# A prefix log-sum-exp over 4 x 4096 rows: other tile heights, another order around the short tiles, other loads by rows

## Chip, core and metric

The kernel runs on one core of one Trainium2 chip. The metric is the device time of one execution in microseconds (us). A profiled execution also has a span: from its first to its last instruction.

## What is computed

The input x has shape (4, 4096, 4128), float32. Along the second axis the output is the running log-sum-exp:

```python
def reference(x):
    B, S, D = x.shape
    out = np.zeros_like(x)
    out[:, 0, :] = x[:, 0, :].copy()
    for t in range(1, S):
        mx = np.maximum(out[:, t - 1, :], x[:, t, :])
        out[:, t, :] = mx + np.log(np.exp(out[:, t - 1, :] - mx) + np.exp(x[:, t, :] - mx))
    return out.astype(np.float32)
```

So out[b, t, d] = log(sum over s <= t of exp(x[b, s, d])).

## The kernel before

**Tiles.** The 4096 rows of each of the 4 batches are cut into tiles of 2 or 3 times 128 rows: partition p of a tile holds 2 or 3 rows that follow one another (`r`), each 4128 numbers wide. The lists `begin` (first batch), `usual` (the two in the middle) and `final` (the last batch) say which tile has how many rows (L176 to L178); there are 46 tiles in all, ten of 2 rows and 36 of 3. A tile lives in one of four SBUF slots (`slots`), in turn, and is worked on in place: loaded, turned into exponentials, into prefix sums, into logarithms, and stored from the same slot.

**Chunks.** A tile's columns are cut into three chunks of 1376. Each chunk goes through these steps; the line is that of the instruction in the profile:

- `exp` (ScalarE, L113): Exp over the chunk's 2 or 3 rows.
- `sums` (VectorE, L133 for 3 rows, L135): the sum of the rows in each partition. For chunks 0 and 1 it goes into a buffer of its own, z0 or z1; for chunk 2 (called passed) it stays in the last row.
- `head` (TensorE, L142): a matmul with a triangular matrix makes, for each partition, the sum of all partitions above it, and of what is carried from the tile before. The result lies in one of two PSUM buffers, in turn.
- `add` (VectorE, L157 and L165, or L160 in a batch's last tile; L150 for chunk 2): adds this to the rows.
- `log` (ScalarE, L173 and L174; L169 for chunk 2): Ln of the rows.
- `fold` (VectorE, L123): brings chunk 2's carry from the tile before into the first row of the next. In a batch's first tile there is none; there `least` (L116) takes a minimum for each of the three chunks, and after a batch's last tile `total` (L126) takes a sum. These feed a check of the number range at the end (L297 to L312), which can send the kernel to a slower general path.

**Order.** The order on each engine is written out by hand, in lists: `act` for ScalarE, `vec` for VectorE, `pe` for TensorE, `move` for the DMA issues, all of them from SP. Each engine works through its list strictly in order. In turn t the ScalarE list has the three Ln of tile t, and the Exps of tile t + 1 placed between them; the VectorE list has the three adds of tile t, with sums of tile t + 1 between them. How many, the pair `turns[t]` says: its first part counts the Exps of tile t + 1 that are placed ahead of Ln 0, ahead of Ln 1, ahead of Ln 2 and behind it; its second part does the same for the sums, ahead of the adds. Where `turns` has no entry the pair is `usual_turn = (0, 2, 3, 3), (0, 0, 1, 1)`. What is not placed ahead comes at the start of the next turn.

**Moves.** SP first issues the loads of tiles 0 to 3. Then, from tile 1 on, each store of a tile t is followed by the load of tile t + 3, which goes into the slot of tile t - 1 and so has to wait until that tile's store has landed. The very last load is issued right behind the last but one. A store waits for the tile's last Ln. A load is one DMA for the whole tile (L93), or, for the tiles chosen by `BY_ROW`, one DMA for each of its rows (L96): before, these are tiles 0 to 6. All loads and stores run on one DMA queue in the order of their issue.

Of the kernel before, what the change touches and what calls it, by code (L numbers as in the profile page):

```python
# [13 lines left out]
MM = 512  # L14
NC = 3
SLOTS = 4
BY_ROW = 7
PASSED = NC - 1
SMALL = 2.0 ** -63
LARGE = 2.0 ** 62  # L20
# [3 lines left out]
def kernel(  # L24
# [57 lines left out]
    class Step:  # L82
# [6 lines left out]
            return rows.rearrange("(p j) d -> p j d", j=self.r)  # L89

        def load(self):
            if self.n >= BY_ROW:
                nc.sync.dma_start(out=self.xt, in_=self.dram(x))  # L93
                return
            for j in range(self.r):
                nc.sync.dma_start(out=self.xt[:, j, :], in_=self.dram(x)[:, j, :])  # L96
# [76 lines left out]
            nc.scalar.activation(e, e, ACT.Ln)  # L173
            nc.scalar.activation(self.row[r - 1], self.z, ACT.Ln)  # L174

    begin = [2, 2, 3, 3, 3, 3, 3, 3, 3, 3, 2, 2]  # L176
    usual = [2, 3, 3, 3, 3, 3, 3, 3, 3, 3, 3]
    final = [2, 3, 3, 3, 3, 3, 3, 3, 3, 2, 2, 2]  # L178
    steps = []
    for b in range(B):  # L180
        row = 0
# [9 lines left out]
    n = len(steps)  # L191
# [3 lines left out]
    for t in range(n):  # L195
# [8 lines left out]
    lists = {"move": moves, "act": [], "vec": [], "pe": []}  # L204
    act, vec, pe = lists["act"], lists["vec"], lists["pe"]
    usual_turn = (0, 2, 3, 3), (0, 0, 1, 1)
    turns = {
# [4 lines left out]
        n - 3: ((0, 0, 3, 3), (0, 0, 0, 0)),  # L212
        n - 2: ((1, 2, 3, 3), (0, 0, 1, 1)),
    }
    given = {"exp": [0] * n, "sums": [0] * n}
# [158 lines left out]
```

## Time and profile before

| what | value |
|---|---|
| median of three timed runs | 1266.24 us (1265.36 to 1266.4) |
| the profiled execution | 1262.61 us |
| its span | 1260.6 us |
| VectorE busy | 1047.2 us, 83% |
| ScalarE busy | 926.1 us, 73% |
| TensorE matmul busy | 601.3 us, 48% |
| read from and written to HBM | 270.53 MB each |
| mean rate of the DMA engines over the span | 429 GB/s |
| DMA issues: stores, whole loads, loads of one row | 46, 39, 19 |

The medians and the profiled execution are different executions of the same program. In the views of the profile, an instruction's line begins with its start and its length in us, or, in groups, with the source line and engine; `out<-in` names what is written and read; `x108` is a count; behind the bar a group has its busy time and the mean of one in ns, and the idle time of the engine before them with what ended it. A waits line reads: who waited for whom, us in total, times, the longest.

### The profile page before, as it was taken

Reading aid. Unit: us, or ns where it says so; the run is one execution under the profiler, and the core shown is the slowest. Engines: PE = TensorE matmul, PEld = TensorE weight load, DVE = VectorE, ACT = ScalarE, POOL = GpSimd, SP = SyncE. Lnnn points to the kernel's source line nnn. Section 1 sums busy time; section 2 is a strip of 40 time slices with the busy share of each in tenths; the row PEclk is TensorE's granted clock in tenths of the full one; section 3 lists DMA queues with packets and bytes.
Section 4 is the critical chain, followed back from the end, with each engine's and each line's share of the span. In section 5 each row is a group of like instructions: output and inputs, shape, how many; then the busy total and the mean of one; then the engine's idle time right before and its main releaser. Section 6 shows DMA issues by size and latency. Waiting matters only on the chain.

```text
span 1260.6 us, 3131 instructions
## 1 busy us (share of the span) xinstructions
PE 601.3 (48%) x830; PEld 233.9 (19%) x830; DVE 1047.2 (83%) x547; ACT 926.1 (73%) x369; POOL 3.8 (0%) x15
## 2 busy tenths in 40 slices
PE   3544444464545444445444544455454454445662
PEld 1221111121222111111111211121121121111220
DVE  4999888895899877888978978888897797888984
ACT  5968777776678677777857777777776677777882
POOL 1000000000000000000000000000000000000000
PEclk9866666676677676666765666666675666666676
DMA  9999999999999999999999999999999999999998
GB/s 398 426 441 427 428 435 434 424 434 431 438 434 429 425 443 434 429 428 436 429 442 428 439 432 428 433 442 429 429 435 426 434 412 442 430 429 433 430 423 375
DMA packets 14994, 541.28 MB, mean 429 GB/s; under 512 B 1664, under 2 KB 1664, under 8 KB 1664
## 3 DMA queue, kind: packets, MB, share of 16 engines
q1 hardware_dynamic: 14976, 541.07, 99.7%
q8 instruction: 7, 0.11, 0.0%
q14 instruction: 11, 0.09, 0.0%
HBM read 270.53 MB, written 270.53 MB: 429 GB/s over the span
## 4 chain that ended last, share of the span: by engine, by line
DMA 61%; ACT 22%; DVE 9%; issue 6%; SPq 1%; ACTq 0%; DVEq 0%
DMA x<-in_x_dram 57%; ACT x L113 11%; ACT x L169 5%; ACT x L173 4%; DMA out_dram<-x 4%; DVE x L150 2%; ACT x L174 2%; DVE x L157 2%; DVE z L135 1%; DVE x L133 1%; DVE z L160 1%; DVE x L135 0%; DVE x L123 0%; SPq L99 0%; DVE short L116 0%
## 5 line engine op out<-in xcount | busy, mean ns | idle before, releaser
L113 ACT ACTIVATE x<-x 128x4128 f32<-128x4128 f32 (+1 forms) x138 | 462.3, 3382 | 183.7 <-DMA x<-in_x_dram 183.6
L142 PE MATMUL p<-z,carried 128*128 128x512 f32 (+1 forms) x504 | 375.2, 910 | 456.4 <-DVE z L135 297.0
L173 ACT ACTIVATE x<-x 128x2752 f32<-128x2752 f32 (+1 forms) x92 | 206.0, 2239 | 129.7 <-DVE z L165 117.1
L133 DVE TENSOR_TENSOR x<-x 128x1376 f32<-128x1376 f32 x108 | 171.2, 1585 | 146.8 <-ACT x L113 146.8
L142 PEld LDWEIGHTS p<-z,carried 128*128 128x128 f32 x504 | 145.8, 309 | 687.4 <-DVE z L135 331.6
L142 PE MATMUL p<-x,summed 128*128 128x512 f32 (+1 forms) x276 | 194.3, 867 | 130.9 <-issue 125.1
L157 DVE TENSOR_TENSOR x<-p,x 128x2752 f32<-128x2752 f32 (+1 forms) x92 | 248.2, 2698 | 0.9 <-PE p L142 0.8
L150 DVE SCALAR_TENSOR_TENSOR x<-p,inner,x 128x4128 f32<-128x4128 f32 (+1 forms) x46 | 193.1, 4198 | 0.6 <-PE p L142 0.5
L135 DVE TENSOR_TENSOR z<-x 127x1376 f32<-127x1376 f32 x92 | 146.3, 1590 | 39.5 <-ACT x L113 33.7
L169 ACT ACTIVATE x<-x 128x4128 f32<-128x4128 f32 (+1 forms) x46 | 155.5, 3379 | 2.4 <-DVE x L150 2.4
L165 DVE TENSOR_TENSOR z<-x 128x1376 f32<-128x1376 f32 x84 | 133.8, 1592 | 2.9
L174 ACT ACTIVATE x<-z 128x1376 f32<-128x1376 f32 x92 | 122.7, 1333 | 0.0
L142 PEld LDWEIGHTS p<-x,summed 128*128 128x128 f32 x276 | 75.3, 290 | 248.5 <-issue 245.9
L135 DVE TENSOR_TENSOR x<-x 128x1376 f32<-128x1376 f32 x46 | 73.2, 1590 | 1.2
L123 DVE TENSOR_TENSOR x<-p,x 1x1376 f32<-1x1376 f32 x42 | 66.1, 1573 | 2.8 <-ACT x L113 2.4
L142 PE MATMUL p<-z,below 128*128 128x512 f32 (+1 forms) x48 | 31.9, 827 | 48.4 <-DVE z L135 28.7
L142 PEld LDWEIGHTS p<-z,below 128*128 128x128 f32 x48 | 12.7, 280 | 66.6 <-issue 31.0
L116 DVE TENSOR_REDUCE short<-x 1x1 f32<-1x1376 f32 x12 | 18.7, 1566 | 0.0
L160 DVE CUSTOM_DVE_ANT_0 z<-x 128x1376 f32<-128x1376 f32 x8 | 12.7, 1592 | 0.3
L126 DVE TENSOR_REDUCE probe<-p 1x1 f32<-1x1376 f32 x4 | 6.3, 1568 | 0.0
L308 PE MATMUL good<-ones,low 128*1 128x1 f32 x2 | 0.2, 164 | 5.5 <-DVE low L306 5.5
L74 POOL MEMSET z<- 128x1376 f32 x2 | 2.5, 1258 | 0.0
(21 smaller groups left out, 4.8 us busy)
## 6 DMA issues: line engine op xcount, KB each, us to landing
out_dram<-x SPq DMA_DIRECT2D x36, 6192.0 KB, 26.0
x<-in_x_dram SPq DMA_DIRECT2D x31, 6192.0 KB, 40.1
out_dram<-x SPq DMA_DIRECT2D x10, 4128.0 KB, 22.0
x<-in_x_dram SPq DMA_DIRECT2D x19, 2064.0 KB, 28.2
x<-in_x_dram SPq DMA_DIRECT2D x8, 4128.0 KB, 34.7
```

The costliest lines, as they stand in the source:

```text
L113: nc.scalar.activation(self.e, self.e, ACT.Exp)
L123: nc.vector.tensor_tensor(out=to, in0=pt[0:1], in1=to, op=ALU.add)
L133: nc.vector.tensor_tensor(out=e[1], in0=e[0], in1=e[1], op=ALU.add)
L135: nc.vector.tensor_tensor(out=self.z[0:n], in0=e[r - 2][0:n], in1=e[r - 1][0:n], op=ALU.add,)
L142: nc.tensor.matmul(self.pt[:, a:b], lhsT=w, rhs=self.z[:, a:b], start=True, stop=True,)
L150: nc.vector.scalar_tensor_tensor(out=self.e, in0=base, scalar=inner[:, 0:1], in1=self.e, op0=ALU.mult, op1=ALU.add,)
L157: nc.vector.tensor_tensor(out=e, in0=base, in1=e, op=ALU.add)
L160: nc.vector.tensor_tensor_reduce(out=self.z, in0=ends[0], in1=ends[1], scale=1.0, scalar=0.0, op0=ALU.add, op1=ALU.add, accum_out=probe[:, ...
L165: nc.vector.tensor_tensor(out=self.z, in0=ends[0], in1=ends[1], op=ALU.add)
L169: nc.scalar.activation(self.e, self.e, ACT.Ln)
L173: nc.scalar.activation(e, e, ACT.Ln)
L174: nc.scalar.activation(self.row[r - 1], self.z, ACT.Ln)
```

## The change

The heights of the tiles are placed otherwise, the engine order gets new entries, and the set of tiles that are loaded by rows changes:

```diff
-BY_ROW = 7
+BY_ROW = (1, 2, 3)
...
-            if self.n >= BY_ROW:
+            if self.n not in BY_ROW:
...
-    begin = [2, 2, 3, 3, 3, 3, 3, 3, 3, 3, 2, 2]
-    usual = [2, 3, 3, 3, 3, 3, 3, 3, 3, 3, 3]
-    final = [2, 3, 3, 3, 3, 3, 3, 3, 3, 2, 2, 2]
+    begin = [2, 3, 3, 3, 3, 3, 3, 3, 3, 3, 3]
+    usual = [3, 3, 3, 3, 3, 2, 3, 3, 3, 3, 3]
+    final = [3, 3, 3, 3, 2, 3, 2, 3, 3, 3, 2, 2]
...
     usual_turn = (0, 2, 3, 3), (0, 0, 1, 1)
+    alone = (0, 0, 0, 0)
     turns = {
-        0: ((2, 3, 3, 3), (0, 0, 1, 1)),
-        1: ((1, 2, 2, 2), (0, 0, 0, 0)),
-        2: ((3, 3, 3, 3), (0, 0, 0, 0)),
-        3: ((2, 2, 3, 3), (0, 0, 0, 0)),
-        n - 3: ((0, 0, 3, 3), (0, 0, 0, 0)),
+        1: ((1, 2, 2, 2), alone),
+        2: ((3, 3, 3, 3), alone),
+        3: ((1, 2, 2, 2), alone),
+        14: ((0, 0, 1, 1), alone),
+        16: ((0, 0, 3, 3), alone),
+        17: ((0, 0, 0, 0), alone),
+        25: ((0, 0, 1, 1), alone),
+        27: ((0, 0, 3, 3), alone),
+        28: ((0, 0, 0, 0), alone),
+        n - 10: ((0, 0, 1, 1), alone),
+        n - 8: ((0, 0, 1, 1), alone),
+        n - 6: ((0, 0, 3, 3), alone),
+        n - 5: ((0, 0, 3, 3), alone),
         n - 2: ((1, 2, 3, 3), (0, 0, 1, 1)),
     }
```

There are now 45 tiles (n = 45), seven of 2 rows and 38 of 3. The 2-row tiles are tile 0, tile 16, tile 27, and, in the last batch, tiles 37, 39, 43 and 44. A batch's first tile has 3 rows, other than the very first. The entry `alone` means that no sums of the next tile are placed ahead in that turn. Tile 0 is loaded by one DMA, tiles 1, 2 and 3 by rows, and all others by one DMA each, so there are 96 DMA issues in place of 104. The instructions of a tile, its slots and the rule by which SP issues loads and stores are as before.

## The prediction

> **What bounds the kernel now.** I read the page first: parts 1 to 3 (engines, DMA share, queues), then the chain of waits, the waits of each engine, the groups by form, and the timelines of SP and ScalarE.
>
> ```profile
> DMA packets 14994, 541.28 MB, mean 429 GB/s; under 512 B 1664, under 2 KB 1664, under 8 KB 1664
> ...
> q1 hardware_dynamic: 14976, 541.07, 99.7%
> ...
> x<-in_x_dram SPq DMA_DIRECT2D x19, 2064.0 KB, 28.2
> ```
>
> One queue carries everything and its 16 engines are busy 99.7% of the span; no compute engine is over 83%. The 19 small issues are the loads by rows of tiles 0 to 6. From SP's timeline I take the pace of the full queue:
>
> ```profile
> 430.65 0.34 SPq L99 DMA_DIRECT2D out_dram<-x  x1
> 431.10 0.37 SPq L93 DMA_DIRECT2D x<-in_x_dram  x1
> 459.89 0.34 SPq L99 DMA_DIRECT2D out_dram<-x  x1
> ...
> 489.14 0.34 SPq L99 DMA_DIRECT2D out_dram<-x  x1
> ```
>
> A store and a load of three rows each leave every 29.245 us. I call one row of 128 partitions (2.114 MB) a unit: 4.874 us. The whole kernel is 256 units, 1247.8 us, and the change moves not one byte of it. The rest of the span is the offset by which a landing lags "units so far x 4.874". The chain of waits (start, us, what) has the landings:
>
> ```profile
> 1.25 11.92 DMA x<-in_x_dram
> ...
> 38.21 24.71 DMA out_dram<-x
> ...
> 135.52 42.05 DMA x<-in_x_dram
> ...
> 195.92 40.71 DMA x<-in_x_dram
> ...
> 322.65 36.51 DMA x<-in_x_dram
> ...
> 431.10 40.12 DMA x<-in_x_dram
> ...
> 743.07 40.12 DMA x<-in_x_dram
> ...
> 860.07 40.66 DMA x<-in_x_dram
> ...
> 1003.25 36.19 DMA x<-in_x_dram
> ```
>
> Start plus length, less units: load 0 (2 units) 13.17 - 9.75 = 3.4; store 0 (12 units) 4.4; load 7 (35) 7.0; load 9 (47) 7.6; load 14 (72) 8.2; load 18 (95) 8.2; load 29 (159) 8.2; load 33 (183) 8.8; load 38 (211) 11.0. So 3.4 us go before the first landing, 4.8 more by 359 us, none from 359 to 783, 2.8 between 783 and 1039. The sum 1247.8 + 11.0 = 1258.8 leaves 1.8 us behind the last landing, to the span of 1260.6. Around the span lie 2.0 us (the profiled execution took 1262.61); the median shown, 1266.24, is 3.6 longer than that execution. I carry the difference between the kernels over to the median.
>
> Compute only has to keep the queue from running dry. Its slack is seen here:
>
> ```profile
> ACT x L113 <- DMA x<-in_x_dram: 183.6, 36, 11.2
> ...
> SPq L99 <- ACT x L169: 1149.7, 45, 31.5
> ```
>
> ScalarE waits about 5 us per tile for a load, and SP waits for the last Ln before each store. The reserve of the queue is what still lies ahead of a store when it is issued: in the steady stretch a load lands 40.1 us after its issue and 29.25 of that is its own store and itself, so 10.9 us. An empty queue needs 2.6: load 0 was issued at 0.80 and landed at 13.17, 12.37 us for 9.75 us of bytes. A reserve under 2.6 leaves a hole, of their difference. The smallest in the middle of the kernel before is store 13's: 77 units x 4.874 + 8.2 - 377.13 = 6.4; the last store's is 254 x 4.874 + 11.0 - 1242.82 = 6.2.
>
> **The change part by part.** (1) *Fewer tiles.* Ten 2-row and 36 3-row tiles become 7 and 38: one store and one load less. Between the landings of loads 18 and 29 (64 units, with one 2-row tile) the clock slipped by 311.97 - 311.95 = 0.02 us. A tile less saves VectorE and ScalarE a few fixed costs that no DMA waits for. Worth 0.05 us.
>
> (2) *Row loads.* 19 become 9 (tiles 1 to 3), 104 DMA issues become 96. In the first stretch the loads of tiles 0 and 1 released these two Exps 9.80 us apart:
>
> ```profile
> 13.26 7.27 ACT L113 ACTIVATE x<-x 128x2752 f32<-128x2752 f32 x3 [11.17 <-DMA x<-in_x_dram]
> ...
> 23.06 4.88 ACT L113 ACTIVATE x<-x 128x2752 f32<-128x2752 f32 x2 [2.54 <-DMA x<-in_x_dram]
> ```
>
> That is 0.026 us per row load above the pace; ten fewer give 0.26 us. The other bound: from 62.92 (12 units) to the Exp at 147.55 that waited for load 6 (29 units) the clock slipped 84.63 - 82.86 = 1.8 us while nine row loads were in the queue, 0.2 each, 1.8 to 2.0 for ten. I take 0.26, because loads 7 and 8, whole ones, also came 30.0 and 29.9 us apart, 0.8 and 0.6 over the pace: the slip is there without row loads.
>
> The Trainium skill (DMA: Bandwidth & Descriptors, Anatomy of one DMA) gives each transfer a fixed cost of about 2.0 us beside its bytes. Laid end to end, 8 transfers fewer would be an estimated 16 us; the flat stretch between loads 18 and 29 shows these costs overlapped.
>
> (3) *The start.* Tile 0's load as one DMA must still bring both rows before the first Exp, so it lands near 13.2. Tile 1 has 3 rows now and lands with unit 5 at 3.5 + 24.4 = 27.9 instead of 23.0. Durations by form:
>
> ```profile
> L113 ACT ACTIVATE x<-x 128x4128 f32<-128x4128 f32 x108 | 388.8, 3632 | 155.2 <-DMA x<-in_x_dram 155.2
> ...
> L157 DVE TENSOR_TENSOR x<-p,x 128x2752 f32<-128x2752 f32 x72 | 216.7, 3010 | 0.4 <-PE p L142 0.4
> ...
> L133 DVE TENSOR_TENSOR x<-x 128x1376 f32<-128x1376 f32 x108 | 171.2, 1585 | 146.8 <-ACT x L113 146.8
> L150 DVE SCALAR_TENSOR_TENSOR x<-p,inner,x 128x4128 f32<-128x4128 f32 x36 | 162.3, 4510 | 0.6 <-PE p L142 0.5
> ```
>
> (Back to back they step about 0.1 us faster, as two Exps of 3.63 in 7.18.) In the new order ScalarE does tile 0's first Ln pair to 29.1, Exps 0 and 1 of tile 1 to 36.2, the second Ln pair to 38.8, Exp 2 of tile 1 to 42.4, the last Ln to 44.8: store 0 leaves at 44.9 instead of 38.2, which costs nothing, since loads to unit 11 land until 57. Behind Exp 2 stands VectorE's chain for tile 1: L123 1.5, L157 2.9, L165 1.6, L133 1.5, L135 1.6, L157 2.9, L165 1.6, L150 4.4 with 0.4 for PE, then the Ln of L169 3.65 and issue 0.3: 42.4 + 22.4 = 64.8. Store 0 is unit 13 and lands at 13 x 4.874 + 4.4 = 67.8. Reserve 3.0 against the needed 2.6: no hole, by 0.4 us. I take 0; one of 2 us if any link slips by 2.4, below zero nothing, as the bytes ahead are fixed. Load 4 waits for store 0 (67.8) with store 1 in front of it until 82. Store 2 follows at about 90.5 against a queue to 96.6, reserve 6; store 3 at 115 against 126, reserve 11.
>
> (4) *The batch's first tile has 3 rows.* VectorE's work for a 3-row tile is 3 x 1.585 + 3 x 1.59 + 1.573 + 2 x 3.01 + 2 x 1.592 + 4.51 = 24.8 us; the minima (3 x 1.566) and the total (1.568) in place of the fold (1.573) make 29.5, against a period of 29.25. The 0.25 over it comes out of the 4.5 us idle in the tile before; the store stays where the load of the next tile sets it.
>
> (5) *2-row tiles inside, with new turns.* A 2-row tile shortens the queue behind the store three tiles earlier by one unit: with the usual order store 14's reserve would be 10.9 - 4.9 = 6. In turn 14 one Exp of tile 15 instead of three stands before the last Ln, and VectorE's ahead-sum is gone, so the store leaves some 7.5 us earlier: reserve about 14. In turn 16 all three Exps of tile 17 stand before tile 16's last Ln; they wait for load 17, then 3 x 3.54 + 2.45 = 13.1 us to the store, and the queue holds store 15 and load 18 (29.25) behind load 17: reserve 29.25 - 13.1 - 0.3, 15 to 16. Worked on in the same way, turns 17 and 18 give 20 and 11, tiles 35 to 43 values of 9 to 18. Hidden by these reserves: 0.
>
> (6) *The end.* 3, 2, 2 in place of 3, 2, 2, 2. SP issues the last load when store 40 has landed and holds store 41 behind that wait; store 41's Ln ends about 3 us after it. From the last landing the chain of Exps, adds and Ln of tiles 43 and 44 gives a last store with 6 us of reserve; before it was 6.2. Worth 0.
>
> Sum: -0.05 - 0.26 = -0.3 us; span 1260.3, median 1265.9. Taken as no change: 0.2% is 2.5 us.
>
> **The rivals.** *A, faster: the slip of batch 0 goes.* If row loads and the uneven start are what moves the offset from 4.4 at 62.92 to 8.2 at 359, the steady pattern from tile 1 on keeps 4.4: -3.8 - 0.3, 1262.1. For it: 359 to 783 is flat. Against: whole loads slipped too, and 783 to 1039 lost 2.8 us with none by rows; those 2.8 may also fall or stay.
>
> *B, slower: a hole behind store 0.* Place: between store 0 and store 1, at about 66 us. It decides from store 1 later than 65.2 on, one us per us. If tile 1's row loads meet the slip of loads 4 to 6 at once (offset 7.6 instead of 3.5), the chain moves by 4.1 us while store 0 has the 4.4 that it is given: 4.1 - 0.4 = 3.7, less 0.3: 1269.6. For it: the narrowest reserve of the kernel, and more 3-row Exps before tile 0's Ln. Against: load 1 landed on the pace before.
>
> *C, slower: a reserve inside or at the end is used up,* through the Exps put ahead of a short tile's Ln (turns 16, 27, n - 6, n - 5) when a load is late; a last store 6.5 us later would cost 6.5 - (6.2 - 2.6) = 2.9: 1268.8.
>
> *D: each DMA has a serial cost.* With 2.6 us for each of 8: 1245. Against it the 0.02 us of (1). One in 100. By the figure of the Trainium skill (DMA: Bandwidth & Descriptors, Anatomy of one DMA) it would be an estimated 16 us, 1250; the trace speaks against it too.
>
> **How the numbers follow.** No change 0.39, A 0.33, D 0.01, B 0.16, C 0.11. Faster 0.34, same 0.39, slower 0.27. The range reaches from A, 1262.0, to B, 1269.8; without the rivals it is 1264 (row loads at their upper bound) to 1268 (a hole of 2 us).
>
> **What would show it.** Steady stores still 29.24 us apart; store 1 near 65 and no dip of the DMA share at 66; store 14 about 10 us behind load 15's landing; a last store with some 6 us of reserve; landings whose offset still climbs in batch 0. It is wrong if that offset stays near 4.4 (A), or jumps at a place where a store comes late (B, C).

## The result and the profile after

The changed kernel takes 1260.86 us (median of 6 runs, 1259.99 to 1261.32), the kernel before in the same comparison 1265.80 us (1264.49 to 1267.01): a ratio of 0.996, interval 0.9948 to 0.9973, or 4.9 us less. The forecast was 1265.9 and no change; the time lies below the range that began at 1262.0. The profiled execution took 1261.23 us with a span of 1259.5; the one of the kernel before, 1262.61 and 1260.6. So the two profiles stand only 1.4 us apart while the medians stand 4.9 apart, and this is a first hint: the profile shown of the kernel before was of an execution 3.2 us quicker than this median, the profile after is of an ordinary one.

From the page of the kernel after, the DMA lines:

```profile
DMA packets 13841, 541.26 MB, mean 430 GB/s; under 512 B 1536, under 2 KB 1536, under 8 KB 1536
...
q1 hardware_dynamic: 13824, 541.07, 99.6%
```

The bytes are the same, the queue is as full as before (99.6 against 99.7%), and there are 1,152 packets fewer. Nothing of a gain is seen on this page. The chain of waits (start, us, what) gives the landings:

```profile
44.70 23.06 DMA out_dram<-x
67.81 29.49 DMA x<-in_x_dram
...
548.12 40.14 DMA x<-in_x_dram
...
949.61 40.12 DMA x<-in_x_dram
```

Store 0 leaves at 44.70 and lands at 67.76; the prediction had 44.9 and 67.8. By the prediction's clock of 4.874 us per unit the offsets are 4.4 (store 0, unit 13), 8.3 (load 21, unit 119) and 10.1 (load 35, unit 201). They climb in batch 0 much as before and end at 10.9, against 12.0 in the first profile of the kernel before (last landing 1259.75, 256 units); that is the whole 1.1 us between the two spans. SP's timeline shows the reserves around the 2-row tile 16 (stores 13 to 17):

```profile
411.23 0.33 SPq L99 DMA_DIRECT2D out_dram<-x  x1
...
432.51 0.33 SPq L99 DMA_DIRECT2D out_dram<-x  x1
...
463.89 0.33 SPq L99 DMA_DIRECT2D out_dram<-x  x1
...
489.31 0.33 SPq L99 DMA_DIRECT2D out_dram<-x  x1
...
508.89 0.33 SPq L99 DMA_DIRECT2D out_dram<-x  x1
```

What lands ahead of store 14 does so at 446.92, so its reserve is 14.4 us (predicted: about 14); store 16's is 16.1 (15 to 16), store 17's 20.9 (20). The order does what it was worked out to do. The question is why this is worth 4.9 us, when the prediction had put it at nothing.

### What a second profile of the kernel before shows

A DMA of this kernel runs on all 16 DMA engines, and the trace keeps the moment at which each of them was done with it: 104 x 16 records before, 96 x 16 after. (The Trainium skill, DMA: Bandwidth & Descriptors, Why a DMA increments its semaphore by 16 and not by 1, says that each engine reports its own share and that only all 16 together mean a landing; the records agree.) A landing is therefore that of the engine furthest behind. The records do not name the engine: "first", "median" and "last" below are taken from the 16 records of a DMA in the order of time. The first engine is far ahead of the last: 0.5 to 0.7 us in the first loads, 2.8 to 5.9 us from load 8 on, up to 6.6 us at the end of the changed kernel.

In a second profile of the kernel before, which took 1266.15 us, SP's and ScalarE's timelines around store 13 read:

```profile
378.02 0.34 SPq L99 DMA_DIRECT2D out_dram<-x  x1
...
402.31 0.34 SPq L99 DMA_DIRECT2D out_dram<-x  x1
...
432.24 0.34 SPq L99 DMA_DIRECT2D out_dram<-x  x1
```

```profile
414.34 7.18 ACT L113 ACTIVATE x<-x 128x4128 f32<-128x4128 f32 x2 [5.33 <-DMA x<-in_x_dram]
...
443.56 7.18 ACT L113 ACTIVATE x<-x 128x4128 f32<-128x4128 f32 x2 [4.82 <-DMA x<-in_x_dram]
```

Store 13 leaves at 378.02, the load ahead of it lands at 384.39 by its last engine, but at 379.59 by its first: the reserve is 6.4 us for the last and 1.6 for the first. The load issued behind this store, load 16, lands at 414.31; from 384.39 it should have taken 6 units, 29.24 us, and took 29.92. Store 15 leaves as much later. Load 17 then comes in step again, 29.22 us behind. Worked from the completion records, the stores with a short reserve in the two profiles of the kernel before, and three stores of the kernel after (us; "loss" is how much later the load behind the store came than its bytes and those of the store allow, counted from the load before it, for the first, the median and the last engine):

```
kernel, store    reserve: last  first    loss of the load behind: first  median  last
before, 2nd   8           6.9    2.8                                0.2     0.2   0.0
before, 2nd  13           6.4    1.6                                1.2     0.9   0.7
before, 2nd  21           7.2    2.2                                0.7     0.1   0.0
before, 2nd  24           6.4    2.0                                0.7     0.8   0.7
before, 2nd  32           6.4    1.3                                1.5     1.2   1.1
before, 2nd  35           6.5    1.7                                0.9     0.9   0.8
before, 2nd  41           6.5    0.8                                1.2     0.0   0.0
before, 1st   8           6.5    3.0                                0.1     0.2   0.2
before, 1st  13           6.4    2.4                                0.3     0.1   0.0
before, 1st  21           6.5    2.7                                0.1     0.0   0.0
before, 1st  24           6.4    2.8                                0.1     0.0   0.0
before, 1st  32           6.2    2.4                                0.3     0.5   0.7
before, 1st  35           6.4    1.5                                1.3     0.9   1.0
before, 1st  41           6.5    1.9                                0.2     0.0   0.0
after        14          14.4   10.3                                0.0     0.1   0.0
after        16          16.1   12.0                                0.0     0.0   0.0
after        35          14.5    8.6                                0.0     0.0   0.0
```

The first engine loses about what its own reserve lacks to 2.7 us: its queue ran dry. (Behind store 41 it takes two loads: load 44 loses 1.2 in the second profile and load 45, issued next, another 0.8; with the reserve of 0.8 that is 2.8.) That is the hole of the prediction, with almost its size (2.6), at another engine. And where it ran dry, more often than not the last engine lost 0.7 to 1.1 us too, though it had 6 us of work queued; load 45 lost 0.6 at the last engine. Store 24 shows that the reserve to the landing does not decide this: it had 6.4 us in both profiles, 2.8 for the first engine in one and 2.0 in the other, and only the latter lost. In the second profile the five losses of the last engine add up to 3.9 us; the kernel after has none of this kind behind the start. The two profiled executions, 1266.15 and 1261.23, stand 4.9 us apart; the other 1 us is not of this kind.

### The profile page after: what moved, and what is told of

The parts are those of the page before. It is cut to its first block, busy times and chain, and to the rows that moved or that the text cites. A ratio compares the mean times of both kernels' runs of the same rounds, so it can differ in the third digit from the quotient of the medians.

```text
span 1259.5 us, 3040 instructions
## 1 busy us (share of the span) xinstructions
PE 576.9 (46%) x812; PEld 224.3 (18%) x812; DVE 1051.9 (84%) x544; ACT 925.5 (73%) x361; POOL 3.8 (0%) x15
## 3 DMA queue, kind: packets, MB, share of 16 engines
q1 hardware_dynamic: 13824, 541.07, 99.6%
## 4 chain that ended last, share of the span: by engine, by line
DMA 61%; ACT 25%; DVE 8%; issue 4%; SPq 0%; ACTq 0%; DVEq 0%
DMA x<-in_x_dram 51%; ACT x L113 13%; DMA out_dram<-x 10%; ACT x L169 5%; ACT x L173 4%; ACT x L174 2%; DVE x L157 2%; DVE x L150 1%; DVE z L165 1%; DVE z L135 1%; DVE x L133 1%; DVE x L123 1%; DVE x L135 0%; SPq L99 0%; DVE z L160 0%
## 5 line engine op out<-in xcount | busy, mean ns | idle before, releaser
L142 PE MATMUL p<-z,carried 128*128 128x512 f32 (+1 forms) x492 | 351.6, 877 | 448.8 <-DVE z L135 303.3
L133 DVE TENSOR_TENSOR x<-x 128x1376 f32<-128x1376 f32 x114 | 180.9, 1587 | 156.1 <-ACT x L113 156.1
L142 PE MATMUL p<-x,summed 128*128 128x512 f32 (+1 forms) x270 | 189.6, 864 | 146.2 <-issue 141.5
L142 PEld LDWEIGHTS p<-z,carried 128*128 128x128 f32 x492 | 136.6, 296 | 665.7 <-DVE z L135 337.0
L157 DVE TENSOR_TENSOR x<-p,x 128x2752 f32<-128x2752 f32 (+1 forms) x90 | 250.8, 2787 | 0.4 <-PE p L142 0.4
L135 DVE TENSOR_TENSOR z<-x 127x1376 f32<-127x1376 f32 x90 | 143.2, 1591 | 20.9 <-ACT x L113 15.8
L165 DVE TENSOR_TENSOR z<-x 128x1376 f32<-128x1376 f32 x82 | 130.6, 1593 | 2.8
L174 ACT ACTIVATE x<-z 128x1376 f32<-128x1376 f32 x90 | 120.0, 1333 | 0.0
L135 DVE TENSOR_TENSOR x<-x 128x1376 f32<-128x1376 f32 x45 | 71.6, 1591 | 1.3
L142 PE MATMUL p<-z,below 128*128 128x512 f32 (+1 forms) x48 | 35.8, 916 | 63.9 <-DVE z L135 42.2
```

The source lines that it names most:

```text
L133: nc.vector.tensor_tensor(out=e[1], in0=e[0], in1=e[1], op=ALU.add)
L135: nc.vector.tensor_tensor(out=self.z[0:n], in0=e[r - 2][0:n], in1=e[r - 1][0:n], op=ALU.add,)
L142: nc.tensor.matmul(self.pt[:, a:b], lhsT=w, rhs=self.z[:, a:b], start=True, stop=True,)
L157: nc.vector.tensor_tensor(out=e, in0=base, in1=e, op=ALU.add)
L165: nc.vector.tensor_tensor(out=self.z, in0=ends[0], in1=ends[1], op=ALU.add)
```

## Experiments

Three theories are set against each other: R, the row loads make the difference; T, the tile list does, with one tile and eight DMA issues fewer; Q, the reserve of the queue at the stores around the short tiles does.

*The kernel before again,* unchanged.

> The kernel before, unchanged, for another profile: the one shown before the prediction took 1262.61 us, while the six timed runs lie at 1264.5 to 1267.0. All theories: 1265.8 +- 0.7 timed, ratio to the kernel before 1.000. If its profiled execution is a typical one, near 1266, the 3 us more must show in the landings as a step of the offset (landing less units x 4.874 us), beyond the 11.0 of the first profile.

Measured: 1266.15 us median, ratio 1.0002 (0.9993 to 1.0011); its profile is the second one above. The longer time does show as steps of the offset, which ends at 15.6, against 12.0 in the first profile: all of the 3.6 us between the two spans.

*Row loads.* In the kernel before, the row loads of the changed one; in the changed one, those of before; and the changed one without any.

```diff
-BY_ROW = 7
+BY_ROW = (1, 2, 3)
...
-            if self.n >= BY_ROW:
+            if self.n not in BY_ROW:
```

> The kernel before with only the set of row loads of the changed kernel (tiles 1 to 3, nine small loads in place of 19). Theory R, the row loads make the difference of 4.9 us: about 1261.5. Theory Q, the reserve of the queue around the short tiles makes it: 1265.5, no more than 0.3 us gained. Theory T, the tile list alone (one tile and 8 DMA issues fewer): 1265.5.

> The changed kernel with the row loads of the kernel before (tiles 0 to 6). Theory R: the gain is lost, about 1265. Theory Q: 1261.2, the gain stays. Theory T: 1261.2.

> The changed kernel with every tile loaded by one DMA, none by rows. If row loads cost what the first bound said (0.026 us each), 0.2 us less: 1260.7; if they shape the start, up to 1 us either way. Theory Q: no store changes its reserve by more than 1 us, so the same within 0.1%.

Measured: 1265.30 us, ratio 0.9995 (0.9986 to 1.0003); 1261.73, 0.9972 (0.9962 to 0.9982); 1260.95, 0.9962 (0.9950 to 0.9974). (In the kernel before tile 1 has 2 rows, so eight row loads are left there, not nine.) Theory R falls from both sides. What rows cost lies within a microsecond: 1261.73 against 1260.86 for eleven more of them (20 in place of 9), 1260.95 against 1260.82 (the changed kernel, measured beside it) for nine fewer.

*The changed kernel without the new turns.*

```diff
-        14: ((0, 0, 1, 1), alone),
...
-        n - 5: ((0, 0, 3, 3), alone),
```

(the ten entries from 14 to n - 5.)

> The changed kernel without the new entries from turn 14 on, so that the usual order runs around the short tiles inside the batches; tile heights and loads as in the changed kernel. Theory Q: reserves of about 6 us come back at stores 14, 25, 35 and 37, and with them most of the 4.9 us: 1264 to 1266. Theory R and theory T: 1261.

Measured: 1264.08 us (1260.83 to 1266.57), ratio 0.9987 (0.9977 to 0.9996). 3.2 of the 4.9 us are gone again. Its profiled execution took 1265.78 us; there stores 14, 17, 25, 28, 35 and 40 left with 6.4 to 6.5 us of reserve, 0.5 to 2.2 for the first engine, and the loads behind the first five lost 0.6 to 1.3 us at the last engine. Behind store 40 the first engine lost 1.6 in load 43, and the last engine 1.5 in load 44. The expectation had named stores 14, 25, 35 and 37; store 37 kept 8.7 us and its load lost nothing at the first engine.

*The kernel before with turns of this kind,* its 46 tiles and its row loads kept; and the same with the row loads of the changed kernel, so that of the change only the tile heights, and the places of the turns that go with them, are missing.

```diff
+        **{t: ((0, 0, 1, 1), (0, 0, 0, 0)) for t in (8, 13, 21, 24, 32, 35, 41)},
```

> The kernel before (its 46 tiles and its row loads) with the entry (0, 0, 1, 1) and no ahead-sums in turns 8, 13, 21, 24, 32, 35 and 41, whose stores left with a reserve of about 6.5 us. Theory Q (a store issued with a reserve of about 6.5 us or less costs the load behind it some 0.8 us on all 16 DMA engines): five to six such losses go, about 1261.5. Theory T (tile list, 45 tiles): 1265.5.

> The kernel before with the seven turn entries of before_turns and the row loads of the changed kernel: all of the change but the tile heights. Theory Q: within 0.1% of before_turns, 1261.5 to 1262.5, one loss of about 1 us being left behind store 14. Theory T: 1265.

Measured: 1261.97 us, ratio 0.9971 (0.9961 to 0.9982); 1262.26, 0.9968 (0.9956 to 0.998). One line of order in the old kernel brings 3.9 of the 4.9 us. Theory T falls as the main cause. In the profile of the first of the two, store 13 leaves at 371.96 and not at 378.02 as in the second profile above:

```profile
371.96 0.34 SPq L99 DMA_DIRECT2D out_dram<-x  x1
```

Load 15 lands at 383.20, so its reserve is 11.2 us, 7.5 for the first engine, and load 16 comes 29.25 us behind load 15. The profile shows one loss of this kind left, of load 17 behind store 14, which now had 5.7 us (1.9 for the first engine): 0.5 last, 1.3 median.

*Late stores made on purpose* in the changed kernel. A few small Exps of a constant into a scrap tile stand ahead of the last Ln in six turns; they change no result, and delay that store alone.

```diff
+        def pause(self):
+            for _ in range(12):
+                nc.scalar.activation(scrap, below.unsqueeze(1).to_broadcast([P, 3, P]), ACT.Exp)
...
+            if c == PASSED and t in (8, 11, 20, 23, 30, 33):
+                act.append(("pause", t, c))
             act.append(("log", t, c))
```

> The changed kernel with seven small idle-work Exps on ScalarE (about 3 us) ahead of the last Ln in turns 8, 11, 20, 23, 30 and 33, nothing else: these six stores leave 3 us later, with a reserve of about 8.4 us in place of 11.4 to the landing of the slowest engine. Theory Q: at most one or two losses, 1261 to 1262. The rule of the prediction (a hole only under 2.6 us): 1261.

> The changed kernel with nine small Exps (4.95 us by the 0.55 us each that the profile showed) in turns 8, 11, 20, 23, 30 and 33: reserve 6.4 us to the slowest engine, 2 to 3 us to the one furthest ahead, which is what the kernel before had at its late stores. Theory Q with the reserve counted from the engine that is furthest ahead (a loss under 2.6 us): three to six losses of 0.8, 1263 to 1266. The same with the reserve counted from the slowest engine (the prediction's rule): 1261.

> The same with twelve such Exps (about 5 us): reserve about 6.3 us, 1 to 3 us for the engine that is furthest ahead. Theory Q: about six losses of 0.8, 1264 to 1266. The rule of the prediction: 1261, since 6.3 is more than 2.6.

> The same with seventeen (about 7 us): reserve about 4.2 us, nothing or less for the engine furthest ahead. Theory Q: six losses of 0.8 to 1.5, 1265 to 1269. The rule of the prediction: 1261, as 4.2 is still more than 2.6.

Each small Exp took 0.55 us, not the 0.42 that I had put for the first three runs, so the delays were 3.8, 5.0, 6.6 and 9.4 us. ScalarE's timeline with seven of them and with twelve, around turn 20 (load 23, behind store 20, is the third row):

```profile
602.52 3.84 ACT L118 ACTIVATE scrap<-below 128x384 f32<-128x384 f32 x7
...
617.51 7.18 ACT L114 ACTIVATE x<-x 128x4128 f32<-128x4128 f32 x2 [4.00 <-DMA x<-in_x_dram]
...
647.14 7.18 ACT L114 ACTIVATE x<-x 128x4128 f32<-128x4128 f32 x2 [0.77 <-DMA x<-in_x_dram]
...
676.38 7.18 ACT L114 ACTIVATE x<-x 128x4128 f32<-128x4128 f32 x2 [4.85 <-DMA x<-in_x_dram]
```

```profile
604.49 6.61 ACT L118 ACTIVATE scrap<-below 128x384 f32<-128x384 f32 x12
...
619.49 7.18 ACT L114 ACTIVATE x<-x 128x4128 f32<-128x4128 f32 x2 [1.23 <-DMA x<-in_x_dram]
...
650.54 7.18 ACT L114 ACTIVATE x<-x 128x4128 f32<-128x4128 f32 x2 [2.19 <-DMA x<-in_x_dram]
...
679.76 7.18 ACT L114 ACTIVATE x<-x 128x4128 f32<-128x4128 f32 x2 [4.83 <-DMA x<-in_x_dram]
```

With seven, load 23 comes 29.63 us behind load 22 (0.4 late, of the last engine only; the first lost 0.0), with twelve 31.05, 1.8 late; load 24 is in step again in both. All four, with the reserves as the records have them:

```
small Exps    time (us)   ratio (interval)           reserve: last   first      loss per late store, first engine
0             1260.82     0.9957 (0.9945 to 0.9969)  11.3 to 12.3   4.3 to 7.7     0
7             1260.75     0.9959 (0.9944 to 0.9974)   7.6 to 8.6    2.2 to 4.0     0.0, one of 0.4
9             1263.83     0.9980 (0.9969 to 0.9991)   6.5 to 7.5    2.0 to 3.2     0.0 to 0.6
12            1268.36     1.0018 (1.0008 to 1.0027)   4.8 to 5.5    0.9 to 1.6     1.1 to 1.8
17            1280.74     1.0118 (1.0100 to 1.0137)   2.0 to 2.1   -2.1 to 0.9     1.9 to 5.0
```

(The profiled execution with nine took 1260.98, at the quick end of its 1260.41 to 1265.29.) Stores 3.8 us late cost nothing here, as five of the six keep 3.2 us or more for the first engine; six stores 6.6 us late cost 7.5 us, 1.3 each, at a reserve of 4.8 to the last engine, where the prediction's rule saw 2 us to spare. Counted from the first engine, the rule holds from 4.0 down to -2.1: in these runs reserve and loss add up to 2.5 to 2.9 wherever there is a loss.

*The changed kernel again:* see the first line of the table.

> The changed kernel, unchanged, beside the next three on one chip. All theories: 1261, ratio 0.996; in its profile no load that all 16 engines finish late, other than the last row load at the start.

## Why the prediction was wrong

- *The bound, the bytes, the pace.* Right: steady stores 29.24 us apart, nothing but the queue sets the time.
- *Step (5), "Hidden by these reserves: 0": wrong, and it is the step that decides.* The new turns were costed for what they might spoil; that the kernel before lost time at its own 6.4 us was ruled out by "A reserve under 2.6 leaves a hole", with a reserve taken to a landing, so to the last of 16 engines. The need of 2.6 was right (2.5 to 2.9 in the runs); it is the first engine's reserve that has to cover it, and that one was 3.5 to 5.7 us shorter. So 6.4 was 0.8 to 3.0, at the edge or under it. From store 3 to the last but one, the new order keeps these reserves at about 10 us and more, and the first engine's at 3.1 and more.
- *"The smallest in the middle of the kernel before is store 13's".* Store 32's was 6.2. I stopped at 6.4 as safe, and left the 2.8 us between 783 and 1039 unexplained. They stand in that profile at loads 33 (0.6), 35 (0.7), 36 (0.8) and 38 (1.0), less 0.3 that load 34 regained, and 35 and 38 are the loads behind two of the stores with such a reserve: the trace held the answer. Of store 35 and loads 37 and 38 it has

```profile
1002.82 0.34 SPq L99 DMA_DIRECT2D out_dram<-x  x1
...
1009.25 7.18 ACT L113 ACTIVATE x<-x 128x4128 f32<-128x4128 f32 x2
...
1039.53 7.18 ACT L113 ACTIVATE x<-x 128x4128 f32<-128x4128 f32 x2 [5.74 <-DMA x<-in_x_dram]
```

Load 37 landed at 1009.23 and load 38 at 1039.45, 30.22 us behind it in place of 29.24.

- *"I carry the difference between the kernels over to the median".* This failed too. The 3.6 us between the profiled execution and the median of before were no constant outside the kernel, but losses in its queue. Between the two profiles 1.3 of them are losses behind late stores (2.6 us in the first, 3.9 in the second); the rest fell mostly in the first loads and at the last engine alone. How far the first engine was ahead decided in each execution which late stores hurt: store 13 had 2.4 us for its first engine in one profile and 1.6 in the other.
- *The end of the sum.* "1247.8 + 11.0 = 1258.8 leaves 1.8 us behind the last landing" took the offset of load 38 for that of the last landing, which was 12.0: 0.9 us are left. The forecast does not rest on this.
- *(2), row loads, and rival A.* The step was right within what can be measured; A had a time near the measured one, 1262.1, for a wrong reason, so that nearness would have been luck. The offset climbs in batch 0 in the changed kernel much as before.
- *(3), rival B.* The step was right, and B did not come: store 1's reserve was 3.5 us (3.0 predicted), when all engines still run within 0.7 us of one another, and load 4 lost 0.4 at the last engine and 0.0 at the first.
- *(1) and D.* Eight issues fewer bring nothing near D's price. (The 2.0 us that is quoted there from the Trainium skill, DMA: Bandwidth & Descriptors, Anatomy of one DMA, is a fit to DMAs issued from GpSimd, while all of these are issued by SP; no run here shows such a cost for each transfer.) What the tile heights bring, beside the turns, is about the 1 us between 1261.97 or 1262.26 and 1260.8; a loss left behind store 14 in the former may be most of it. No run tells these apart.
- *(4).* No run tries the batch's first tile alone.
- *(6), rival C.* The step was right, and C did not come: the last store had 7.2 us (6 predicted). The first engine had 0.7 there, and nothing comes behind that store.

## What to carry to other kernels

Where one full DMA queue sets the time, ask how much work lies queued when the next transfer is issued, and count it from the DMA engine that is furthest ahead, not from the landing: the spread between the engines (here 3 to 6.6 us) is taken off the reserve. An order of instructions that lets some outputs leave a few microseconds sooner was worth 3.9 us here, without one instruction made cheaper. And look at the profile of a second execution where the shown one differs from the median by as much as the effect in question.

## What the runs showed of the hardware

- When the first engine of a DMA ran dry, the last one mostly lost 0.6 to 1.3 us too, in the load behind, though it had 6 us of work queued (4.8 with twelve small Exps). In load 16 of the second profile (store 13), 16 packets of 49,536 bytes that begin between 407.2 and 408.9, near its end, take 2.2 to 3.2 us where the median packet takes 1.829; loads 27 and 35 have 18 and 20 of them. Sixteen would be one for each engine, but the packets do not name it. Why is open.
- The last of the first row loads shows such a loss too: first, median and last engine lost 0.6 us in the row load ahead of store 0 in the kernel after, with 12.6 us of reserve at the first engine, and 0.4 to 0.7 in the kernel before. So a short reserve is not its only occasion.
- Beside this, now and then a load comes 0.4 to 1.2 us late at the last engine alone, the median not moved (loads 23, 32 and 41 of the changed kernel, 0.8 to 1.0 each). They are about as common in both kernels and make most of the climb of the offset from 4.4 to 10.9 that the changed kernel has left. They are not all chance: a second profile of the changed kernel has them at the same three loads with the same sizes. Packets of instructions begin at 623, 890 and 1126, shortly ahead of each, but others pass without a loss; what they are was not tried.
- With six stores made late by nine small Exps, the executions of one program spread over 5 us (1260.4 to 1265.3), without any over 2.4 us (1260.0 to 1262.4).
